# A state-space layer's small tables made on GpSimd instead of VectorE

## The chip, the cores and the metric

One core of a Trainium2 chip runs the whole kernel. TensorE (PE; PEld is its weight load) multiplies, VectorE (DVE) and ScalarE (ACT) do elementwise work, GpSimd (POOL) does little in the kernel before, and SyncE (SP) issues most DMAs; ACT and POOL issue some too. The metric is the device time of one execution in microseconds (us), the median of the runs.

## The reference

Two layers of a streaming encoder over 256 frames of 2048 channels: a diagonal state-space layer (S5), a gated MLP with a causal convolution, attention with a compressed K/V, and a second MLP. The change touches the first of them. Cut to that:

```python
def s5_mixer(u, a_re, a_im, log_dt, b_re, b_im, c_re, c_im, d_skip, w_glu, b_glu):
    dt = exp(log_dt)                        # one per group; 128 groups of 16 channels
    ab = exp(dt * a_re) * (cos(dt * a_im), sin(dt * a_im))   # 64 complex states per group
    bb = (ab - 1) / a * b
    # per group: x_t = bb u_t;  h_t = ab h_{t-1} + x_t;  y_t = Re(c h_t) + d_skip u_t
    y = gelu(y)
    val, gate = split(y @ w_glu + b_glu)    # w_glu is 2048 x 4096
    return val * sigmoid(gate)

h = rmsnorm(x, norm_g[0, 0]);  x = x + rmsnorm(s5_mixer(h, ...), norm_g[0, 1])
```

All arithmetic is float32 (products of weights as a high and a low part, so that each weight tile is split first: `whi` by ScalarE, `wlo` by VectorE).

## The kernel before

`s5` treats the 256 frames as 32 chunks of 8. Within a chunk the recurrence is a small matrix per group; from chunk to chunk a scan runs over the state. The 128 groups go in 16 blocks of 8 groups, and a loop of 18 rounds (`for n in range(nb + 2)`) pipelines the blocks: in round n, block n is prepared (`part_k`, `part_e`), block n - 1 has its scan (`part_v`, `part_r`, `part_h`) and block n - 2 gives its output (`part_c`). Four blocks make a quarter. At the end of a quarter `part_d` takes the Gelu, and a list `todo` of early GLU units (1 MB of weights each, `glu_early`) is worked off by `advance` between the parts.

What the change touches:

- `scale_x(rs, qt)`: x of quarter qt. VectorE multiplies both halves by the norm's weights `gX` (L369), ScalarE then by the rows' norms `rs` into `Xn` (L373). x lies in two tiles of the tag `raw`, into which the first two GLU weight units are loaded later (L84).
- `powers(qt)`: for a quarter's 32 groups, the eight powers of the complex step `L`, three doublings of four VectorE instructions each (L396 to L399) in the tile `z`; ScalarE then writes the signed copies `zs` (L401 to L404).
- `product` (L453): `zs` times the weights `bc` of a block, four 128x1024 VectorE instructions, two for `e` and two for `f`. The two of e are added by an accumulating DMA that POOL issues (L467).
- `frames(k)`: phase tables of two blocks. VectorE reduces the angle (L411 to L413), ScalarE takes Abs, Sin and Sin (L414 to L416). `part_r` and `part_h` multiply by them.
- the skip weights `dB` times a mask (L352), which `part_k` adds (L437).
- `rstd` (L117): the first norm; POOL takes the power -0.5 (L121).
- `lead_e(n)` and `lead_f(n)` make e and f of a block one or two rounds ahead. At the end of round n stand `lead_f(n + 1)` and `lead_e(n + 2)`.

Each engine works through its own queue in order. A scheduler sets the order when the program is built, from the order of the code and modelled times; `behind(ins)` places what is written in it behind the instruction `ins` of the same engine. A tile with a tag shares its tag's buffers, so an instruction also waits for the buffer's last reader.

Of the kernel before, what the change touches and what calls it, by code (L numbers as in the profile page):

```python
# [11 lines left out]
AF = mybir.ActivationFunctionType  # L12
# [3 lines left out]
P = 128  # L16
# [30 lines left out]
def tile_trunk(ctx: ExitStack, tc: tile.TileContext, a: dict):  # L47
# [69 lines left out]
    def rstd(tot, width, n):  # L117
        ms = T(sp, [P, width], F32, "rs_ms")
        dve.tensor_scalar(ms, tot, 1.0 / n, EPS, op0=ALU.mult, op1=ALU.add)
        y = T(sp, [P, width], F32, "rs_y")  # L120
        pool.tensor_tensor(y, ms, eps_half[:, :width], op=ALU.pow)  # L121
# [62 lines left out]
    def behind(ins):  # L184
        return nullcontext() if ins is None else tc.issue_after(ins)
# [96 lines left out]
    def s5(f):  # L282
        with tc.tile_pool(name="s5", bufs=2) as q1, tc.tile_pool(name="dr", bufs=2, space=bass.MemoryType.DRAM) as dr:
            w0 = env["wp"]
            dt = T(q1, [P, P], F32, "dt", 1)
            sA = T(q1, [P, 2, P], F32, "sA", 1)
            sync.dma_start(sA, a["sA"])
            sync.dma_start(dt, a["sL"].partition_broadcast(P))
            sync.dma_start(cst, a["cst"])
            X = [T(w0, [P, 4, 512], F32, "raw") for _ in range(2)]  # L290
            for k in range(8):
# [60 lines left out]
            dve.tensor_tensor(  # L352
                dB.rearrange("p (g q) -> p g q", q=16),
                dB.rearrange("p (g q) -> p g q", q=16),
                dmask.unsqueeze(1).to_broadcast([P, 32, 16]),
                op=ALU.mult,
            )

            def first_norm():
                pst = wk()  # L360
# [2 lines left out]

            Xn = [T(aa, [P, 8, P], F32, f"act{q}") for q in range(4)]

            def scale_x(rs, qt):
                c = slice(P * qt, P * qt + P)
                for h in range(2):
                    dve.tensor_tensor(  # L369
                        X[h][:, :, c], X[h][:, :, c], gX[:, c].unsqueeze(1).to_broadcast([P, 4, P]), op=ALU.mult  # L370
                    )
                for s in range(8):
                    act.activation(  # L373
                        Xn[qt][:, :, 16 * s : 16 * s + 16],
                        X[s // 4][:, s % 4, c].rearrange("p (g q) -> p g q", q=16),
                        AF.Copy,
                        scale=rs[:, s : s + 1],
                    )

            def powers(qt):  # L380
                ps_ = slice(32 * qt, 32 * qt + 32)
                z = T(q1, [P, 2, 9, 2, 32], F32, "z", 1)
                pool.memset(z[:, 0, 8, 1, :], 1.0)
                pool.memset(z[:, 1, 8, 1, :], 0.0)
                act.activation(z[:, :, 8, 0, :], cf[:, :, ps_], AF.Copy)
                act.activation(z[:, :, 0, 1, :], L[8][:, :, ps_], AF.Copy)
                for k, o, i, m in ((1, 7, 8, 1), (2, 5, 7, 2), (4, 1, 5, 4)):

                    def v(b):
                        return z[:, :, b : b + m].rearrange("p c m t n -> p c (m t) n")  # L390

                    def l(c):
                        return L[k][:, c, ps_].unsqueeze(1).unsqueeze(1).to_broadcast([P, 2, 2 * m, 32])

                    u, w = (T(q1, [P, 2, 8, 32], F32, n, 1)[:, :, : 2 * m, :] for n in ("pu", "pw"))
                    dve.tensor_tensor(u, v(i), l(0), op=ALU.mult)  # L396
                    dve.tensor_tensor(w, v(i), l(1), op=ALU.mult)
                    dve.tensor_tensor(v(o)[:, 0], u[:, 0], w[:, 1], op=ALU.subtract)
                    dve.tensor_tensor(v(o)[:, 1], u[:, 1], w[:, 0], op=ALU.add)  # L399
                zz = T(q1, [P, 4, 8, 32], F32, "zs")  # L400
                act.activation(zz[:, 1], z[:, 1, 0:8, 1, :], AF.Copy, scale=cst[:, C_SG : C_SG + 1])  # L401
                act.activation(zz[:, 2], z[:, 0, 1:9, 0, :], AF.Copy, scale=cst[:, C_NSG : C_NSG + 1])
                act.activation(zz[:, 3], z[:, 1, 1:9, 0, :], AF.Copy, scale=-1.0)
                act.activation(zz[:, 0], z[:, 0, 0:8, 1, :], AF.Copy)  # L404
                return zz

            def frames(k):
                ps_ = slice(FR * NP * k, FR * NP * (k + 1))
                m, n = T(q1, [P, FR * NP, 32], F32, "si"), T(q1, [P, FR * NP, 32], F32, "co")
                cv = cst[:, C_CV : C_CV + 32].unsqueeze(1).to_broadcast([P, FR * NP, 32])  # L410
                dve.tensor_tensor(m, th[:, ps_].unsqueeze(2).to_broadcast([P, FR * NP, 32]), cv, op=ALU.mult)  # L411
                dve.tensor_scalar(n, m, MAGIC, MAGIC, op0=ALU.add, op1=ALU.subtract)
                dve.tensor_tensor(m, m, n, op=ALU.subtract)  # L413
                act.activation(n, m, AF.Abs)  # L414
                act.activation(m, m, AF.Sin, scale=cst[:, C_TPI : C_TPI + 1])
                act.activation(n, n, AF.Sin, bias=half_pi, scale=-TWO_PI)  # L416
                return [z.rearrange("p (k n) c -> k p (n c)", k=FR) for z in (m, n)]

            FR = 2
# [41 lines left out]
            def lead_e(n):  # L461
                if n >= nb:
                    return
                if n % PB == 0:
                    zs[n // PB] = powers(n // PB)
                E[n], e2 = product("e1", 3, n, 0), product("e2", 2, n, 1)
                pool.dma_start(E[n], e2, accum_op=ALU.add)  # L467

            def lead_f(n):
                if n >= nb:  # L470
                    return
                F[n] = product("f1", 3, n, 2), product("f2", 3, n, 3)
                if n % FR == 0:
                    si, co = frames(n // FR)
                    for k in range(FR):
                        fr[n + k] = (si[k], co[k])

# [30 lines left out]
            def part_e(e1):  # L508
                ET = T(q1, [P, NP, P], F32, "ET", 1)
                for w in range(NG):  # L510
                    ptv = wk().rearrange("p (g t) -> p g t", g=4)
                    for g in range(4):
                        pe.transpose(ptv[:, g, :], e1[:, 4 * w + g].rearrange("p s q -> p (s q)"), ident)
                    act.activation(ET[:, 4 * w : 4 * w + 4, :], ptv, AF.Copy)
                return ET

            def part_v(U, ET):
# [80 lines left out]
            def advance(steps):  # L598
                for _ in range(steps):
                    while todo and next(todo[0], True) is True:  # L600
                        todo.pop(0)

            rs = first_norm()
            for n in range(3):
                fetch(n, sync)
            lead_e(0)
            lead_f(0)
            scale_x(rs, 0)
            for n in range(nb + 2):
                if 0 <= n - 1 < nb:  # L610
                    vs = part_v(U[n - 1], ET.pop(n - 1))
                if n >= 2:
                    m = n - 2
                    if m % PB == 0:
                        yg = T(q1, [P, 8, P], F32, "yg", 1)
                    part_c(m, yg, F.pop(m), U.pop(m), TP.pop(m), H.pop(m))
                if 0 <= n - 1 < nb:
                    R = part_r(n - 1, vs, *fr[n - 1])
                if n < nb:
                    U[n], TP[n] = part_k(n, F[n], bc.pop(n))  # L620
                    fetch(n + 3, act)
                    ET[n] = part_e(E.pop(n))
                if n > nb:
                    advance(2)
                if n >= 2 and m % PB == PB - 1:
                    part_d(m // PB, yg)
                    todo.append(glu_steps(m // PB))
                if n <= nb:
                    advance(2)
                    if n == nb:  # L630
                        tiny = T(sp, [P, 1], F32, "tot")
                        act.activation(tiny, half_pi, AF.Gelu_apprx_tanh)
# [12 lines left out]
        return todo  # L645
# [595 lines left out]
```

## Time and profile before

| | |
|---|---|
| time, median of 3 runs | 2130.54 us (2128.49 to 2135.25) |
| profiled execution | 2132.15 us, of which the span is 2130.4 us |
| TensorE busy | 2048.3 us (96%) |
| VectorE busy | 1375.3 us (65%) |
| ScalarE busy | 1092.4 us (51%) |
| GpSimd busy | 31.4 us (1%) |
| granted TensorE clock, mean | 0.991 |

The span runs from the first to the last instruction. A row of a timeline reads: start, length (of all if "xN" stands behind), engine and line, operation, output<-inputs with their shapes, and in brackets the idle time of the engine ahead of it and what ended that. A row of groups has the number of instructions, then busy us in all, mean ns of one, and idle time. A row of waits has who waited <- for whom, then us in all, times, and the longest.

### The profile page before, as it was taken

Reading aid. Unit: us, or ns where it says so; the run is one execution under the profiler, and the core shown is the slowest. Engines: PE = TensorE matmul, PEld = TensorE weight load, DVE = VectorE, ACT = ScalarE, POOL = GpSimd, SP = SyncE. Lnnn points to the kernel's source line nnn. Section 1 sums busy time; section 2 is a strip of 40 time slices with the busy share of each in tenths; the row PEclk is TensorE's granted clock in tenths of the full one; section 3 lists DMA queues with packets and bytes.
Section 4 is the critical chain, followed back from the end, with each engine's and each line's share of the span. In section 5 each row is a group of like instructions: output and inputs, shape, how many; then the busy total and the mean of one; then the engine's idle time right before and its main releaser. Section 6 shows DMA issues by size and latency. Waiting matters only on the chain.

```text
span 2130.4 us, 30733 instructions
## 1 busy us (share of the span) xinstructions
PE 2048.3 (96%) x12372; PEld 1755.5 (82%) x12372; DVE 1375.3 (65%) x1931; ACT 1092.4 (51%) x1676; POOL 31.4 (1%) x73
## 2 busy tenths in 40 slices
PE   3789999999999999999999999999999999999998
PEld 2567788988888888888878998898888888888886
DVE  8889677665466556656685666666546655665567
ACT  6565456554455345434464555555445544553444
POOL 1000000000000000000000000000000000000000
PEclk9899999999999999999999999999999999999999
DMA  5768775455655565555564344445555556555554
GB/s 149 202 182 212 247 249 167 154 184 183 201 188 185 190 198 183 181 190 197 197 198 149 124 139 165 168 161 186 179 200 194 185 185 201 182 193 182 198 190 147
DMA packets 292255, 392.15 MB, mean 184 GB/s; under 512 B 10256, under 2 KB 205456, under 8 KB 291600
## 3 DMA queue, kind: packets, MB, share of 16 engines
q1 hardware_dynamic: 285632, 374.45, 53.4%
q0 software_dynamic: 2304, 8.39, 2.3%
q10 hardware_dynamic: 4176, 7.34, 1.0%
q8 instruction: 97, 1.59, 0.3%
q14 instruction: 46, 0.38, 0.1%
HBM read 375.73 MB, written 6.03 MB: 179 GB/s over the span
## 4 chain that ended last, share of the span: by engine, by line
PE 85%; DVE 6%; DMA 4%; ACT 2%; issue 1%; SPq 0%; POOL 0%; ACTq 0%; DVEq 0%; POOLq 0%
PE wk L757 29%; PE wk L759 15%; PE acc L114 9%; PE acc L113 9%; PE acc L112 9%; PE wk L112 2%; PE wk L113 2%; PE wk L114 2%; PE wk L430 2%; PE acc L254 2%; PE acc L253 2%; PE acc L256 1%; DVE wlo L76 1%; ACT junk L139 1%; PE acc L193 1%
## 5 line engine op out<-in xcount | busy, mean ns | idle before, releaser
L76 DVE TENSOR_TENSOR wlo<-raw,whi 128x1024 fp32r<-128x1024 f32 (+1 forms) x606 | 719.4, 1190 | 568.1 <-ACT whi L75 562.9
L75 ACT ACTIVATE whi<-raw 128x1024 fp32r<-128x1024 f32 (+1 forms) x606 | 622.6, 1030 | 708.2 <-PE wk L757 311.3
L757 PE MATMUL wk<-act,whi 128*128 128x512 f32 x2688 | 673.7, 392 | 0.0
L757 PEld LDWEIGHTS wk<-act,whi 128*128 128x128 f32 x2688 | 484.0, 189 | 86.9
L759 PEld LDWEIGHTS wk<-act,wlo 128*128 128x128 f32 x2688 | 366.7, 190 | 26.2
L759 PE MATMUL wk<-act,wlo 128*128 128x256 f32 x2688 | 374.8, 282 | 0.0
L114 PE MATMUL acc<-whi,hl 128*128 128x512 f32 x652 | 255.9, 394 | 0.0
L113 PE MATMUL acc<-wlo,hh 128*128 128x512 f32 x652 | 255.8, 392 | 0.0
L112 PE MATMUL acc<-whi,hh 128*128 128x512 f32 x652 | 253.5, 389 | 0.0
L113 PEld LDWEIGHTS acc<-wlo,hh 128*128 128x128 f32 x652 | 122.4, 188 | 28.3 <-DVE wlo L76 0.2
L112 PEld LDWEIGHTS acc<-whi,hh 128*128 128x128 f32 x652 | 122.4, 188 | 27.5 <-ACT hh L75 0.5
L114 PEld LDWEIGHTS acc<-whi,hl 128*128 128x128 f32 x652 | 122.6, 188 | 24.7
L816 DVE SCALAR_TENSOR_TENSOR cv<-gs,cw,cv 128x255 f32<-128x255 f32 (+1 forms) x168 | 81.0, 482 | 17.2 <-ACT cv L814 14.3
L814 ACT ACTIVATE cv<-gs,cb,cw 128x256 f32<-128x256 f32 x84 | 49.9, 594 | 45.9 <-DVE gs L765 45.9
L253 PE MATMUL acc<-whi,act 128*128 128x512 f32 x156 | 65.3, 419 | 3.9 <-ACT act L75 3.8
L254 PE MATMUL acc<-whi,act 128*128 128x512 f32 x156 | 63.1, 404 | 1.2 <-DVE act L76 1.2
L113 PE MATMUL acc<-wlo,act 128*128 128x512 f32 (+1 forms) x152 | 54.6, 359 | 0.1
L112 PE MATMUL acc<-whi,act 128*128 128x512 f32 (+1 forms) x152 | 54.0, 357 | 0.0
L114 PE MATMUL acc<-whi,act 128*128 128x512 f32 (+1 forms) x152 | 53.9, 356 | 0.0
L112 PE MATMUL wk<-x,whi 128*128 128x256 f32 x160 | 47.2, 297 | 2.3 <-ACT x L75 2.3
L256 PE MATMUL acc<-wlo,act 128*128 128x512 f32 x156 | 49.1, 397 | 0.0
L76 DVE TENSOR_TENSOR x<-raw,x 128x1024 fp32r<-128x1024 f32 x30 | 36.0, 1221 | 16.2 <-ACT x L75 16.2
(306 smaller groups left out, 2503.3 us busy)
## 6 DMA issues: line engine op xcount, KB each, us to landing
raw<-in_w_gate SPq DMA_DIRECT2D x88, 1024.0 KB
raw<-in_w_up SPq DMA_DIRECT2D x88, 1024.0 KB
raw<-in_w_down SPq DMA_DIRECT2D x88, 1024.0 KB
raw<-in_w_glu SPq DMA_DIRECT2D x21, 1024.0 KB
x<-in_w_glu SPq DMA_DIRECT2D x11, 1024.0 KB
raw<-in_w_o SPq DMA_DIRECT2D x9, 1024.0 KB
e<-e POOLq DMA_DIRECT2D x16, 512.0 KB, 6.1
TP<-kd SPq DMA_DIRECT2D x64, 128.0 KB
```

Source lines behind the costliest of these rows:

```text
L75: act.activation(hi, src, AF.Copy)
L76: (eng or dve).tensor_tensor(lo, src, hi.bitcast(F32), op=ALU.subtract)
L112: pe.matmul(o, lh, rh, start=first, stop=False)
L113: pe.matmul(o, lh, rl, start=False, stop=False)
L114: pe.matmul(o, ll, rh, start=False, stop=last)
L253: pe.matmul(bank, ah, wh[:, k, :], start=first and k == 0, stop=False)
L254: pe.matmul(bank, al, wh[:, k, :], start=False, stop=False)
L256: pe.matmul(bank, acts(tb, 4 * b + j + k)[0], wl[:, k, :], start=False, stop=last and k == hk - 1)
L757: pe.matmul(o, w, pair(kt), start=kt == 0, stop=False)
L759: pe.matmul(o[:, 0, :], w, pair(kt)[:, 0], start=False, stop=kt == KT - 1)
L814: act.activation(cv[:, ft, :], gv[:, ft, :], AF.Identity, scale=cw[:, 2, n : n + 1], bias=cb[:, n : n + 1])
L816: dve.scalar_tensor_tensor(cv[:, ft, sh:], gv[:, ft, : S - sh], cw[:, 2 - sh, n : n + 1], cv[:, ft, sh:], op0=ALU.mult, op1=ALU.add,)
```

## The change

- The phase tables' angles (`angles`, from L411 to L413), the powers of quarters 1 to 3 counted from 0, and the multiplication of x by `gX` for those quarters go to POOL, and so does the mask of the skip weights. Quarter 0's powers and multiplication stay on VectorE.
- On POOL they are placed behind the last accumulating DMA issued so far (`env["trig"]`; the first two tables behind nothing, what follows them behind the norm's power).
- The first two tables are made ahead of the norm. Otherwise angles are made in `lead_f`, and ScalarE's sines for them in `lead_r`, a round later; powers of a quarter are made in rounds 0, 2 and 6, ScalarE's copies (`signs`) in rounds 2, 6 and 10, behind the last copy of ET.
- ScalarE scales quarters 1, 2 and 3 of x in rounds 2, 3 and 4, before in rounds 0 and 1.
- The tiny Gelu that is written near the end of the layer (it loads ScalarE's table) is placed behind the last sine.
- The step `dt` is loaded ahead of `sA`.

The diff, cut to its core:

```diff
-        pool.tensor_tensor(y, ms, eps_half[:, :width], op=ALU.pow)
+        env["trig"] = pool.tensor_tensor(y, ms, eps_half[:, :width], op=ALU.pow).ins
...
+            sync.dma_start(dt, a["sL"].partition_broadcast(P))
             sync.dma_start(sA, a["sA"])
-            sync.dma_start(dt, a["sL"].partition_broadcast(P))
...
+            def gain_x(qt, eng):
+                c = slice(P * qt, P * qt + P)
+                with behind(env["trig"] if eng is pool else None):
+                    for h in range(2):
+                        z = X[h][:, :, c]
+                        eng.tensor_tensor(z, z, gX[:, c].unsqueeze(1).to_broadcast([P, 4, P]), op=ALU.mult)
...
-            def powers(qt):
+            def powers(qt, eng):
...
-                    dve.tensor_tensor(u, v(i), l(0), op=ALU.mult)
-                    dve.tensor_tensor(w, v(i), l(1), op=ALU.mult)
-                    dve.tensor_tensor(v(o)[:, 0], u[:, 0], w[:, 1], op=ALU.subtract)
-                    dve.tensor_tensor(v(o)[:, 1], u[:, 1], w[:, 0], op=ALU.add)
+                    eng.tensor_tensor(u, v(i), l(0), op=ALU.mult)
+                    eng.tensor_tensor(w, v(i), l(1), op=ALU.mult)
+                    eng.tensor_tensor(v(o)[:, 0], u[:, 0], w[:, 1], op=ALU.subtract)
+                    eng.tensor_tensor(v(o)[:, 1], u[:, 1], w[:, 0], op=ALU.add)
+                return z
...
-            def frames(k):
+            def angles(k):
...
-                dve.tensor_tensor(m, th[:, ps_].unsqueeze(2).to_broadcast([P, FR * NP, 32]), cv, op=ALU.mult)
-                dve.tensor_scalar(n, m, MAGIC, MAGIC, op0=ALU.add, op1=ALU.subtract)
-                dve.tensor_tensor(m, m, n, op=ALU.subtract)
+                with behind(env.get("trig")):
+                    pool.tensor_tensor(m, th[:, ps_].unsqueeze(2).to_broadcast([P, FR * NP, 32]), cv, op=ALU.mult)
+                pool.tensor_scalar(n, m, MAGIC, MAGIC, op0=ALU.add, op1=ALU.subtract)
+                pool.tensor_tensor(m, m, n, op=ALU.subtract)
+                return m, n
...
-                pool.dma_start(E[n], e2, accum_op=ALU.add)
+                env["trig"] = pool.dma_start(E[n], e2, accum_op=ALU.add).ins
...
+            an = {k: angles(k) for k in range(2)}
             rs = first_norm()
+            with behind(env["trig"]):
+                skips = dB.rearrange("p (g q) -> p g q", q=16)
+                pool.tensor_tensor(skips, skips, dmask.unsqueeze(1).to_broadcast([P, 32, 16]), op=ALU.mult)
+            gain_x(1, pool)
+            gain_x(2, pool)
...
+                        with behind(env["sin"]):
+                            act.activation(tiny, half_pi, AF.Gelu_apprx_tanh)
...
+                if n % PB == 2 and n + 2 < nb:
+                    zs[n // PB + 1] = signs(z)
                 lead_e(n + 2)
-                if n < 2:
-                    scale_x(rs, n + 1)
+                if n == 0 or n % PB == 2 and n + 6 < nb:
+                    z = powers((n + 6) // PB, pool)
                 if n == 1:
-                    scale_x(rs, 3)
+                    gain_x(3, pool)
+                if 1 < n < 5:
+                    scale_x(rs, n - 1)
```

The order that results, at three places. Row: line, operation, output<-inputs, shape; numbers behind names count tiles. The lines of the changed kernel are some 20 higher. First POOL's queue after the memsets at the program's start, before:

```order
L121 TENSOR_TENSOR rs_y_205<-rs_ms_203,cst_73 128x8
L383 MEMSET z_577 128x32
L384 MEMSET z_577 128x32
L467 DMA e_71_247<-e_72_249 128x1024
L467 DMA e_86_323<-e_87_325 128x1024
L467 DMA e_90_332<-e_91_334 128x1024
```

And the same place now:

```order
L414 TENSOR_TENSOR si_200<-th_179,cst_73 128x512
L414 TENSOR_TENSOR si_205<-th_179,cst_73 128x512
L415 TENSOR_SCALAR co_201<-si_200 128x512
L415 TENSOR_SCALAR co_206<-si_205 128x512
L416 TENSOR_TENSOR si_200<-si_200,co_201 128x512
L416 TENSOR_TENSOR si_205<-si_205,co_206 128x512
L121 TENSOR_TENSOR rs_y_214<-rs_ms_212,cst_73 128x8
L615 TENSOR_TENSOR dB_107<-dB_107,cst_73 128x512
L365 TENSOR_TENSOR raw_96<-raw_96,gX_106 128x4x128
L365 TENSOR_TENSOR raw_97<-raw_97,gX_106 128x4x128
L365 TENSOR_TENSOR raw_96<-raw_96,gX_106 128x4x128
L365 TENSOR_TENSOR raw_97<-raw_97,gX_106 128x4x128
```

Two tables now stand ahead of the norm's power, and the skip weights and two quarters of x between it and the first DMA of e. Next VectorE, from the last steps of the first norm to the first product, before:

```order
L127 TENSOR_TENSOR rs_r_211<-rs_t_207,rs_y_205 128x8
L399 TENSOR_TENSOR z_219<-pu_230,pw_231 128x128
L369 TENSOR_TENSOR raw_97<-raw_97,gX_106 128x4x128
L396 TENSOR_TENSOR pu_236<-z_219,L_34_148 128x512
L397 TENSOR_TENSOR pw_237<-z_219,L_34_148 128x512
L369 TENSOR_TENSOR raw_96<-raw_96,gX_106 128x4x128
L398 TENSOR_TENSOR z_219<-pu_236,pw_237 128x256
L399 TENSOR_TENSOR z_219<-pu_236,pw_237 128x256
L369 TENSOR_TENSOR raw_97<-raw_97,gX_106 128x4x128
L453 TENSOR_TENSOR f_73_252<-zs_242,bc_213 128x1024
```

And the same end now:

```order
L127 TENSOR_TENSOR rs_r_220<-rs_t_216,rs_y_214 128x8
L396 TENSOR_TENSOR z_233<-pu_238,pw_239 128x64
L397 TENSOR_TENSOR z_233<-pu_238,pw_239 128x64
L394 TENSOR_TENSOR pu_244<-z_233,L_33_147 128x2x128
L395 TENSOR_TENSOR pw_245<-z_233,L_33_147 128x2x128
L396 TENSOR_TENSOR z_233<-pu_244,pw_245 128x128
L397 TENSOR_TENSOR z_233<-pu_244,pw_245 128x128
L394 TENSOR_TENSOR pu_250<-z_233,L_34_148 128x512
L395 TENSOR_TENSOR pw_251<-z_233,L_34_148 128x512
L396 TENSOR_TENSOR z_233<-pu_250,pw_251 128x256
L397 TENSOR_TENSOR z_233<-pu_250,pw_251 128x256
L459 TENSOR_TENSOR f_77_266<-zs_256,bc_227 128x1024
```

Of the multiplications by `gX` none stands here any more, and the norm's end stands earlier among the powers. Last ScalarE at its start (L632 is the tiny Gelu; L139 the squares of x for the norm), before:

```order
L306 ACTIVATE dt_91<-dt_91 128x128
L632 ACT_TABLE_LOAD
L632 ACTIVATE tot_2761<-cst_73 128x1
L311 ACT_TABLE_LOAD
L311 ACTIVATE mag_117<-e_18_115 128x128
L312 ACTIVATE mag_20_118<-e_18_115 128x128
L139 ACTIVATE junk_122,xst_21_121<-raw_96 128x512
```

And now:

```order
L306 ACTIVATE dt_91<-dt_91 128x128
L139 ACTIVATE junk_122,xst_21_121<-raw_96 128x512
L311 ACTIVATE mag_117<-e_18_115 128x128
L312 ACTIVATE mag_20_118<-e_18_115 128x128
L139 ACTIVATE junk_124,xst_21_121<-raw_96 128x512
```

Two table loads have left the start; the Gelu's now stands behind the sines of the last table.

More of the change, by code (lines that the diff above doesn't have):

```diff
@@ L351, in s5 @@
             dmask = cst[:, C_DM : C_DM + 16]
[L352 to L357, printed above, removed]
             def first_norm():
@@ L378, in scale_x @@
                     )
-            def powers(qt):
+            def powers(qt, eng):
                 ps_ = slice(32 * qt, 32 * qt + 32)
                 z = T(q1, [P, 2, 9, 2, 32], F32, "z", 1)
-                pool.memset(z[:, 0, 8, 1, :], 1.0)
+                with behind(env["trig"] if eng is pool else None):
+                    pool.memset(z[:, 0, 8, 1, :], 1.0)
                 pool.memset(z[:, 1, 8, 1, :], 0.0)
@@ L395, in powers, with signs @@
                     u, w = (T(q1, [P, 2, 8, 32], F32, n, 1)[:, :, : 2 * m, :] for n in ("pu", "pw"))
[L396 to L399, printed above, removed]
-                zz = T(q1, [P, 4, 8, 32], F32, "zs")
[L401 to L404, printed above, removed]
+                    eng.tensor_tensor(u, v(i), l(0), op=ALU.mult)
[3 more added lines that the diff above has]
+                return z
+            def signs(z):
+                zz = T(q1, [P, 4, 8, 32], F32, "zs")
+                with behind(env.get("et")):
+                    act.activation(zz[:, 1], z[:, 1, 0:8, 1, :], AF.Copy, scale=cst[:, C_SG : C_SG + 1])
+                    act.activation(zz[:, 2], z[:, 0, 1:9, 0, :], AF.Copy, scale=cst[:, C_NSG : C_NSG + 1])
+                    act.activation(zz[:, 3], z[:, 1, 1:9, 0, :], AF.Copy, scale=-1.0)
+                    act.activation(zz[:, 0], z[:, 0, 0:8, 1, :], AF.Copy)
                 return zz
-            def frames(k):
+            def angles(k):
                 ps_ = slice(FR * NP * k, FR * NP * (k + 1))
@@ L472, in lead_f, with lead_r @@
                 F[n] = product("f1", 3, n, 2), product("f2", 3, n, 3)
-                if n % FR == 0:
-                    si, co = frames(n // FR)
+                if n % FR == 0 and n // FR > 1:
+                    an[n // FR] = angles(n // FR)
+            def lead_r(n):
+                if n < nb and n % FR == 0:
+                    si, co = frames(*an.pop(n // FR))
                     for k in range(FR):
@@ L513, in part_e @@
                         pe.transpose(ptv[:, g, :], e1[:, 4 * w + g].rearrange("p s q -> p (s q)"), ident)
-                    act.activation(ET[:, 4 * w : 4 * w + 4, :], ptv, AF.Copy)
+                    env["et"] = act.activation(ET[:, 4 * w : 4 * w + 4, :], ptv, AF.Copy).ins
                 return ET
@@ L601, in advance @@
                         todo.pop(0)
+            an = {k: angles(k) for k in range(2)}
             rs = first_norm()
+            with behind(env["trig"]):
[3 more added lines that the diff above has]
+            gain_x(2, pool)
             for n in range(3):
                 fetch(n, sync)
+            zs[0] = signs(powers(0, dve))
             lead_e(0)
             lead_f(0)
+            gain_x(0, dve)
             scale_x(rs, 0)
@@ L622, in s5 @@
                     ET[n] = part_e(E.pop(n))
+                    lead_r(n)
                 if n > nb:
```

10 lines of the change are left out of this document (2 added, 8 removed).

## Prediction

> **What bounds the kernel now.** I read the head of the page first, then a table of busy time by stage, then who waited for whom in the stage that the change touches.
>
> ```profile
> span 2130.4 us, 30733 instructions
> PE 2048.3 (96%) x12372; PEld 1755.5 (82%) x12372; DVE 1375.3 (65%) x1931; ACT 1092.4 (51%) x1676; POOL 31.4 (1%) x73
> ```
>
> Over the whole span TensorE is the bound: it is idle for 2130.4 - 2048.3 = 82.1 us in all, and no change on other engines can win more than that. The stage table (columns after the stretch: its length, then busy us and instructions of PE, PEld, DVE, ACT, POOL, the granted clock, DMA share, GB/s) shows where these idle us lie.
>
> ```profile
> 0.00:25.40 25.40, 0.59 (x2) 0.50 (x2) 18.97 (x57) 18.49 (x45) 3.30 (x17) 1.00 0.48 157
> 25.40:60.00 34.60, 21.57 (x296) 15.60 (x300) 30.58 (x49) 16.92 (x51) 3.84 (x6) 0.90 0.71 178
> 60.00:100.00 40.00, 28.07 (x346) 21.14 (x339) 34.47 (x56) 23.99 (x47) 3.66 (x6) 0.83 0.69 185
> 100.00:126.00 26.00, 24.84 (x360) 20.65 (x358) 24.98 (x35) 18.15 (x39) 1.92 (x4) 1.00 0.73 191
> 126.00:140.00 14.00, 9.10 (x101) 7.28 (x99) 8.10 (x12) 5.86 (x11) 0.86 (x1) 0.94 0.69 178
> 140.00:200.00 60.00, 55.67 (x707) 44.09 (x708) 59.54 (x98) 38.93 (x72) 3.48 (x4) 0.96 0.76 204
> 200.00:235.00 35.00, 35.00 (x431) 28.56 (x431) 27.23 (x42) 16.32 (x31) 1.01 (x3) 1.00 0.61 169
> ```
>
> All of the change lies in these 235 us (the state-space layer with the early GLU units), and so do 60.2 of the 82.1 us: 24.8, 13.0, 11.9, 1.2, 4.9, 4.3 and 0. VectorE is the engine to look at: it is busy for 157.7 of the 174.6 us from 25.4 to 200, and for all but 1.5 us of the two stretches 100 to 126 and 140 to 200, while POOL does almost nothing. After 200 TensorE has no idle time and VectorE has some: there nothing is to be won.
>
> The waits of TensorE in this stage name VectorE (the steps of R, H and f), but also ACT at the start:
>
> ```profile
> PE wk L482 <- ACT act L373: 6.3, 1, 6.3
> PE wk L545 <- DVE R L540: 6.3, 3, 5.3
> PE wk L430 <- DVE H L554: 5.5, 1, 5.5
> PE wk L430 <- DVE f L453: 4.6, 2, 2.8
> PE wk L513 <- DMA e<-e: 2.6, 1, 2.6
> ```
>
> **What leaves VectorE.** These groups are the phase tables (L411 to L413), the powers (L396 to L399), x times its gain (L369) and the skip weights (L352):
>
> ```profile
> L396 DVE TENSOR_TENSOR pu<-z,L 128x128 f32<-128x128 f32 (+2 forms) x12 | 5.6, 464 | 0.1
> L397 DVE TENSOR_TENSOR pw<-z,L 128x128 f32<-128x128 f32 (+2 forms) x12 | 5.6, 464 | 0.0
> L411 DVE TENSOR_TENSOR si<-th,cst 128x512 f32<-128x512 f32 x8 | 5.4, 685 | 0.0
> L369 DVE TENSOR_TENSOR raw<-raw,gX 128x512 f32<-128x512 f32 x8 | 5.4, 685 | 0.0
> L413 DVE TENSOR_TENSOR si<-si,co 128x512 f32<-128x512 f32 x8 | 5.4, 680 | 0.0
> L398 DVE TENSOR_TENSOR z<-pu,pw 128x64 f32<-128x64 f32 (+2 forms) x12 | 3.7, 308 | 0.1
> L399 DVE TENSOR_TENSOR z<-pu,pw 128x64 f32<-128x64 f32 (+2 forms) x12 | 3.7, 306 | 0.0
> L412 DVE TENSOR_SCALAR co<-si 128x512 f32<-128x512 f32 x8 | 3.3, 420 | 0.0
> L352 DVE TENSOR_TENSOR dB<-dB,cst 128x512 f32<-128x512 f32 x1 | 0.7, 686 | 0.0
> ```
>
> Tables 0 and 1 stand ahead of VectorE's wait for ScalarE's first sines:
>
> ```profile
> 9.44 1.29 DVE L411 TENSOR_TENSOR si<-th,cst 128x512 f32<-128x512 f32 x2
> 12.62 0.43 DVE L321 TENSOR_TENSOR L<-L,mag 128x256 f32<-128x256 f32 x1
> ```
>
> All tables: 14.1 us. Three quarters of the powers: 0.75 x 18.6 = 14.0 us. Six of eight multiplications by the gain: 4.1. With the skip weights that makes 32.9 us in 24 + 36 + 6 + 1 = 67 instructions. Tables 0 and 1 (a quarter of 14.1, 3.5 us) are made before 12.62 us, inside that wait, and save nothing: 29.4 us in 61 instructions remain. Instructions that follow each other overlap by some 0.08 us (two products take 2.35 us in the next fence, not twice 1.22), so the room that VectorE gains is 29.4 - 61 x 0.08, about 24.5 us.
>
> **What it costs on POOL.** No row shows large arithmetic on POOL. Its memsets do show a fixed part and a rate:
>
> ```profile
> 0.74 0.31 POOL L651 MEMSET krE<- 128x256 f32 x1 [0.29 <-POOLq L1231]
> 1.83 0.12 POOL L383 MEMSET z<- 128x32 f32 x1
> 19.58 1.76 POOL L121 TENSOR_TENSOR rs_y<-rs_ms,cst 128x8 f32<-128x8 f32 x1 [17.50 <-DVE rs_ms L119]
> 27.84 2.35 DVE L453 TENSOR_TENSOR e<-zs,bc 128x1024 f32<-128x1024 f32 x2
> 35.55 1.97 PE L513 MATMUL wk<-cst,e 128*128 128x128 f32 x8 [2.55 <-DMA e<-e]
> ```
>
> That is (0.31 - 0.12) / 224 = 0.85 ns an element and about 0.1 us. A tensor_tensor moves three streams where a memset moves one. So the lower bound of a 128x512 one is 0.53 us, as one stream, and the upper, three streams in turn, 1.4 us (a tensor_scalar 0.97). The moved work is 67 instructions with 12288 elements per partition in tables, 3 x 2688 in powers, 3072 in gains and 512: 23936. Lower bound 6.7 + 20.3 = 27 us; upper 6.7 + 0.85 x (3 x 19840 + 2 x 4096) = 64 us. I take a value near the upper, 55 us, since two reads and a write are nearer to three streams than to one. The power of L121 is another operation and no price for a product.
>
> [...]
>
> POOL has the room: it is busy for 18 of the 235 us. Behind the moved work in its queue stand the sixteen accumulating DMAs of e. The powers of a quarter, some 7 us, stand ahead of one of them. TensorE waited for an e only once, 2.6 us at the first; the others land ahead of use. I cost this at nothing; the cover is that lead, and were it gone, up to 7 us would be lost in each of three quarters. ScalarE's sines come a round later, still ahead of the product that reads them: nothing again. That x is kept longer (ScalarE scales quarter 3 three rounds later) moves the first two 1 MB loads of GLU weights, which are loaded into the tiles of x. In the run before, they stand right behind a TP transfer that then takes long:
>
> ```profile
> 47.52 2.44 SPq L502 DMA_DIRECT2D TP<-kd  x4
> 50.07 3.28 SPq L84 DMA_DIRECT2D raw<-in_w_glu  x2
> 49.38 8.91 DMA TP<-kd
> 127.34 10.08 DMA bc<-in_sBC
> ```
>
> This collision goes and comes back a round or two later, where every round has one (the wait for bc at 127 is such a case, and stays): nothing, with 4 us to either side in the range.
>
> **Where the room on VectorE turns into time.** Start: of the six multiplications by the gain that stand ahead of the first products of e, two remain: 4 x 0.6 = 2.4 us, and the first transposes of e at 35.55 follow: -2.4. I count nothing for the two table loads that leave ScalarE's start (it then waits for POOL's first table), nor for the swapped first loads, a few tenths. From 25.4 to 100 some 8 of the 24.5 us go, in a chain that passes from VectorE to TensorE, ScalarE and the TP transfer and back; TensorE is idle for 24.9 us there, and I take half of the 8: -4. From 100 to 200 some 12 us go, but TensorE is idle for only 1.2 + 4.3 = 5.5 us beside the wait for bc, which caps it; I take -4. The tail: the Gelu table is loaded earlier, out of the path:
>
> ```profile
> 235.29 1.28 ACT L581 ACT_TABLE_LOAD   x1
> 237.27 1.18 PE L585 MATMUL wk<-cst,yg 128*128 128x128 f32 x8 [0.85 <-ACT yg L581]
> ```
>
> TensorE's wait there is 0.85 us: -1 with what follows it. Sum: -2.4 - 4 - 4 - 1 = -11.4 us, from the profiled execution's 2132.15 to 2120.7. That execution is 1.6 us above the median of 2130.54, so in terms of the median 2119.
>
> **The row on which the sign hangs.** Do POOL and VectorE get in each other's way? There is one kind of row that tells: POOL's small power beside VectorE instructions.
>
> ```profile
> 1383.46 1.21 DVE L76 TENSOR_TENSOR wlo<-raw,whi 128x1024 fp32r<-128x1024 f32 x1
> 1383.68 1.39 POOL L147 TENSOR_TENSOR rs_y<-tot,cst 128x1 f32<-128x1 f32 x1 [16.03 <-DVE tot L145]
> 1384.65 1.21 DVE L76 TENSOR_TENSOR wlo<-raw,whi 128x1024 fp32r<-128x1024 f32 x1
> 1390.43 0.54 POOL L147 TENSOR_TENSOR rs_y<-tot,cst 128x1 f32<-128x1 f32 x1 [5.31 <-DVE tot L145]
> ```
>
> The same instruction takes 0.54 us alone and 1.39 us when it begins inside a VectorE instruction with two SBUF inputs: it ends 0.40 us after that one. So they do exclude each other, and here POOL gave way: both VectorE instructions keep their 1.21 us. My forecast reads this as the rule: POOL, which has time, fits into VectorE's pauses and its PSUM reads.
>
> [...]
>
> **Rivals.** (1) VectorE waits for whole POOL instructions, and the kernel gets slower. Place: from 21 us (skip weights and gains beside the first powers) to 200. Price: VectorE loses 0.9 of POOL's time (its busy share, 157.7 of 174.6) and wins 24.5. Without the first two tables, of which most runs before 12.6 us, POOL has 24 to 56 us: between -3 and +26 us on VectorE. At my 55 us, 48 remain: +19, of which the chain's pauses before 100 us take up some 7: +12, so 2142.5. It decides from the point where a 128x512 instruction on POOL holds VectorE for longer than about 0.65 us, what VectorE needs for it.
> (2) The relief is hidden: TensorE runs at 93 to 96% from 100 us on, the TP and bc transfers set the rounds before, and the start gains nothing, since rs then comes late. Only the tail and 1 or 2 us remain: 2127. For it speaks that the biggest single wait (bc, 10.08 us) is a DMA's; against it that VectorE is busy without a break for 100 us.
> (3) VectorE really was behind most of TensorE's idle time: all but the 4.9 us around the bc wait of the 35.3 us from 25.4 to 200 shrinks by two thirds, with start and tail: -24, so 2107.
>
> **How the numbers follow.** Forecast 0.38 (its own range 2113 to 2124); rival 1 0.27; rival 2 0.25; rival 3 0.10. A difference within 0.3%, 6.4 us, is about what cannot be told from no change. Faster is forecast and rival 3, with a hundredth from rival 2: 0.49. Slower is rival 1 but for two hundredths: 0.25. Same is the rest: 0.26. The range reaches from 2106 (rival 3) to 2143 (rival 1 at its taken price), which leaves out its upper half and the rest of rival 3, below 0.2.
>
> **What would show it.** Right: the stretch up to the last early part (235 us now) shorter by about 10 us, VectorE below 90% from 100 to 200, its products still 1.22 us and following each other at 1.13, POOL's 128x512 instructions long (over 1 us) and stretched by waiting. Wrong by rival 1: products or wlo well above 1.22 us, or gaps between them that end with POOL. Wrong by rival 2: VectorE with more idle time and TensorE's waits unchanged, now on TP, bc or ACT. A late e or a late first weight would show as a new wait of TensorE for L513, or of ScalarE for raw.

## The result: 1.2% slower

The changed kernel takes 2156.01 us (median of 2154.83 to 2157.94) against 2130.21 us before in runs beside it: a ratio of 1.0116, 95% interval 1.0101 to 1.0132. The forecast was 2119, a gain. The change loses 25.8 us, and the time lies 13 us beyond rival 1.

The head of the page of the changed kernel:

```profile
span 2153.3 us, 30743 instructions
PE 2054.5 (95%) x12372; PEld 1762.1 (82%) x12372; DVE 1387.1 (64%) x1864; ACT 1087.3 (50%) x1672; POOL 117.2 (5%) x140
```

VectorE has 67 instructions fewer, which took 32.9 us, and yet is busy for 11.8 us more (1387.1 against 1375.3): the rest of its work has grown by some 44.7 us. POOL has gained 85.8 us, where 55 were reckoned.

TensorE works off the same 12372 matmuls. Of the 22.9 us by which the profiled span is longer (2153.3 against 2130.4), 16.7 are its idle time (98.8 against 82.1) and 6.2 its busy time (2054.5 against 2048.3); its mean granted clock is 0.985, before 0.991. The sum of the prediction had no term for the clock.

Four of the seven stages, in the cuts of the prediction:

```profile
60.00:100.00 40.00, 26.23 (x418) 20.46 (x406) 38.73 (x41) 22.97 (x54) 28.38 (x25) 0.83 0.77 197
100.00:126.00 26.00, 23.95 (x282) 18.79 (x280) 21.92 (x26) 16.06 (x32) 6.62 (x9) 0.87 0.66 169
126.00:140.00 14.00, 10.33 (x86) 8.42 (x90) 14.00 (x14) 7.53 (x14) 13.84 (x13) 0.76 0.75 209
140.00:200.00 60.00, 47.00 (x534) 36.79 (x527) 45.64 (x59) 30.56 (x58) 13.63 (x10) 0.91 0.62 161
```

From 60 to 100 us VectorE is now busier (38.73 of 40 us, before 34.47) with fewer instructions (41, before 56). From 126 to 140 VectorE and POOL have no pause between them: 14.00 and 13.84 of 14 us. From 140 to 200 TensorE loses 8.7 us (47.00, before 55.67), and there VectorE is not full. The granted clock is lower in the last three rows than in the same stretches before: 0.87, 0.76 and 0.91, where it was 1.00, 0.94 and 0.96. Apart from the clock, two things are to be told from each other: stretched instructions, and something else that delays TensorE late in the layer.

Which instructions grew, from the groups of VectorE in the first 300 us (busy us, then mean ns of one, then idle time before them):

```profile
L459 DVE TENSOR_TENSOR f<-zs,bc 128x1024 f32<-128x1024 f32 x32 | 45.4, 1420 | 0.2 <-ACT zs L404 0.2
L76 DVE TENSOR_TENSOR wlo<-raw,whi 128x1024 fp32r<-128x1024 f32 x30 | 43.8, 1466 | 11.1 <-ACT whi L75 10.9
L542 DVE TENSOR_TENSOR w<-w,w 128x256 f32<-128x256 f32 x16 | 12.8, 801 | 0.1
L540 DVE TENSOR_TENSOR w<-wk,co 128x256 f32<-128x256 f32 x16 | 6.7, 416 | 4.4 <-PE wk L538 4.4
L279 DVE TENSOR_TENSOR f<-acc,f 128x512 f32<-128x512 f32 x24 | 16.5, 687 | 13.4 <-PE acc L256 13.4
```

The same groups before:

```profile
L453 DVE TENSOR_TENSOR f<-zs,bc 128x1024 f32<-128x1024 f32 x32 | 38.9, 1217 | 0.8 <-PE wk L430 0.8
L76 DVE TENSOR_TENSOR wlo<-raw,whi 128x1024 fp32r<-128x1024 f32 x32 | 39.0, 1221 | 8.2 <-ACT whi L75 8.1
L534 DVE TENSOR_TENSOR w<-w,w 128x256 f32<-128x256 f32 x16 | 6.7, 421 | 0.1
L532 DVE TENSOR_TENSOR w<-wk,co 128x256 f32<-128x256 f32 x16 | 6.7, 421 | 6.1 <-PE wk L530 6.1
L279 DVE TENSOR_TENSOR f<-acc,f 128x512 f32<-128x512 f32 x24 | 16.5, 687 | 8.6 <-PE acc L256 8.6
```

Instructions with both operands in SBUF (f from zs and bc, wlo, w from w and w) grew by 17%, 20% and 90%. Those with one operand in PSUM (`wk`, `acc` are PSUM tiles) kept their length to within 0.005 us: 416 against 421 ns, 687 against 687. In order of time it looks like this (start, duration, both in us; `x4` is four instructions in a row, with the length of all four):

```profile
24.22 5.75 POOL L365 TENSOR_TENSOR raw<-raw,gX 128x512 f32<-128x512 f32 x4
24.41 1.22 DVE L124 TENSOR_TENSOR rs_t<-rs_t,rs_ms 128x8 f32<-128x8 f32 x1
25.75 1.22 DVE L125 TENSOR_SCALAR rs_t<-rs_t 128x8 f32<-128x8 f32 x1
...
59.54 2.82 POOL L365 TENSOR_TENSOR raw<-raw,gX 128x512 f32<-128x512 f32 x2
59.89 2.76 DVE L542 TENSOR_TENSOR w<-w,w 128x256 f32<-128x256 f32 x1
```

At 59.89 an addition that takes 0.42 us before takes 2.76 and ends 0.29 us after POOL's two multiplications. An instruction of eight elements per partition takes 1.22 us beside POOL's multiplications (24.41 and 25.75), before 0.16. Here it is VectorE that gives way.

The second suspect is in the waits of the first 300 us (total us, times, longest):

```profile
ACT co L420 <- POOL si L416: 25.4, 6, 6.0
PE wk L490 <- ACT act L370: 10.3, 1, 10.3
PE wk L553 <- DVE R L548: 9.3, 3, 4.1
PE wk L521 <- ACT yg L574: 7.7, 2, 4.8
PE wk L521 <- ACT U L492: 4.5, 2, 4.4
```

ScalarE waits 25.4 us for POOL's tables, six times. In its queue its copies for `yg` and `U` stand behind that `Abs` (L420), and TensorE then waits 7.7 and 4.5 us for them. How the wait arises can be seen at 153:

```profile
153.14 0.87 POOL L471 DMA_DIRECT2D e<-e  x1 [12.68 <-issue]
153.70 1.62 POOL L414 TENSOR_TENSOR si<-th,cst 128x512 f32<-128x512 f32 x1
155.41 2.78 POOL L415 TENSOR_SCALAR co<-si 128x512 f32<-128x512 f32 x1
158.27 1.26 POOL L416 TENSOR_TENSOR si<-si,co 128x512 f32<-128x512 f32 x1
159.57 0.63 ACT L420 ACTIVATE co<-si 128x512 f32<-128x512 f32 x1 [5.99 <-POOL si L416]
```

The table stands in POOL's queue behind the trigger of an accumulating DMA that POOL issues only at 153.14, then takes 5.8 us, and ScalarE has come to it 6 us too early.

### The profile page after: what moved, and what is told of

Read it like the earlier page. It is cut to its first block, busy times and chain, and to the rows that moved or that the text cites. A ratio compares the mean times of both kernels' runs of the same rounds, so it can differ in the third digit from the quotient of the medians.

```text
span 2153.3 us, 30743 instructions
## 1 busy us (share of the span) xinstructions
PE 2054.5 (95%) x12372; PEld 1762.1 (82%) x12372; DVE 1387.1 (64%) x1864; ACT 1087.3 (50%) x1672; POOL 117.2 (5%) x140
## 4 chain that ended last, share of the span: by engine, by line
PE 83%; DVE 4%; DMA 2%; ACT 2%; issue 1%; SPq 0%; POOL 0%; ACTq 0%; DVEq 0%; POOLq 0%
PE wk L779 28%; PE wk L781 15%; PE acc L114 9%; PE acc L113 9%; PE acc L112 9%; PE wk L112 2%; PE wk L113 2%; PE wk L114 2%; PE acc L253 1%; PE acc L254 1%; DVE wlo L76 1%; PE acc L256 1%; DMA bias<-in_b_glu 1%; PE wk L256 1%; PE acc L193 1%
## 5 line engine op out<-in xcount | busy, mean ns | idle before, releaser
L147 POOL TENSOR_TENSOR rs_y<-tot,cst 128x1 f32<-128x1 f32 x18 | 12.8, 713 | 1914.1 <-DVE tot L145 1190.9
```

## Experiments

Three theories. T1: VectorE and POOL keep each other out of SBUF, so that VectorE loses more than the moved work gave it. T2: the stretch is harmless, and ScalarE's wait in its queue for POOL's tables is the loss. T3: the new order alone (sines a round later, x scaled later, Gelu table, first loads) is the loss.

**All arithmetic back on VectorE, the new order kept** (all_dve). The edit, on the changed kernel, cut to its lines:

```diff
-                with behind(env.get("trig")):
-                    pool.tensor_tensor(m, th[...], cv, op=ALU.mult)
-                pool.tensor_scalar(n, m, MAGIC, MAGIC, op0=ALU.add, op1=ALU.subtract)
-                pool.tensor_tensor(m, m, n, op=ALU.subtract)
+                dve.tensor_tensor(m, th[...], cv, op=ALU.mult)
+                dve.tensor_scalar(n, m, MAGIC, MAGIC, op0=ALU.add, op1=ALU.subtract)
+                dve.tensor_tensor(m, m, n, op=ALU.subtract)
...
-            gain_x(1, pool)
-            gain_x(2, pool)
+            gain_x(1, dve)
+            gain_x(2, dve)
...
-                    z = powers((n + 6) // PB, pool)
+                    z = powers((n + 6) // PB, dve)
```

> The changed kernel with all of its POOL arithmetic put back on VectorE (tables, powers, gains, skip weights); the new order, the later sines, the Gelu table's place and the swapped first loads stay. Theory 1 (VectorE and POOL exclude each other, the stretch of VectorE's instructions is the loss) and theory 2 (ScalarE waits in its queue for POOL's tables) both expect 2124 to 2131 us, at or a little below the kernel before, with products back at 1.22 us. Theory 3 (the new order itself costs: x kept longer, first GLU weights later) expects more than 2140.

Measured: 2131.21 us, ratio to before 1.0005 (0.9991 to 1.002). T3 falls: the new order costs nothing that can be measured, and gains nothing.

**Only the tables back on VectorE** (angles_dve: the first half of that diff), and **only the tables on POOL** (angles_only: its second half).

> Only the phase tables go back to VectorE; powers, gains and skip weights stay on POOL. POOL then has 45 of its 86 us of moved work. Theory 1 expects about half of the loss to stay, 2138 to 2146 us, with products still stretched. Theory 2 (ScalarE's waits for tables, 25.4 us in six) expects the whole loss but the start's part to be gone: 2130 to 2136.

> Only the phase tables stay on POOL (41 of the 86 us); powers, gains and skip weights go back to VectorE. Theory 1 expects 2138 to 2146 us. Theory 2 expects ScalarE's waits to stay near 20 us and the time near 2150.

Measured: 2140.79 us, ratio 1.0053 (1.0036 to 1.007), with powers, gains and skip weights on POOL; 2156.07 us, ratio 1.013 (1.0105 to 1.0154), with the tables alone. The tables by themselves give a loss as large as the whole change, the rest 9 us; the two parts do not add up (24 + 9 against 25). ScalarE's wait for POOL is 23.9 us in angles_only and absent in angles_dve, so these two runs still fit T2 for the larger part, but not T2 alone: angles_dve has no such wait and is slower all the same. T1's 2138 to 2146 holds for angles_dve and is missed by 10 us for angles_only.

**The start back on VectorE** (start_dve).

```diff
-            an = {k: angles(k) for k in range(2)}
+            an = {k: angles(k, dve) for k in range(2)}
...
-            gain_x(1, pool)
-            gain_x(2, pool)
+            gain_x(1, dve)
+            gain_x(2, dve)
```

(The skip weights go back too.)

> The changed kernel with the work ahead of the first round on VectorE again: the first two tables, the skip weights and the gains of quarters 1 and 2. The first transposes of e came 7.1 us later with the change (42.64 against 35.55 us). If that delay runs through to the end, the time falls by 6 to 9 us to 2147 to 2150, and the first transposes come before 36. If it is taken up by later waits, the time stays within 2 us of 2156.

Measured: 2149.03 us, ratio 1.009 (1.0074 to 1.0106), 7 us less than the changed kernel. In all these kernels the transposes of e (eight per block, 128 in all) are a mark of how far the layer has come. Their row in the view by source line gives count, shortest/median/longest ns, and the first and last start; one row each of before, changed, all_dve, angles_dve, angles_only and start_dve:

```profile
L513 PE MATMUL wk<-cst,e x128: 272/273/473, 35.6 to 220.1; 128*128 128x128 f32 x128
```
```profile
L521 PE MATMUL wk<-cst,e x128: 272/273/477, 42.6 to 244.5; 128*128 128x128 f32 x128
```
```profile
L520 PE MATMUL wk<-cst,e x128: 272/273/477, 41.7 to 218.0; 128*128 128x128 f32 x128
```
```profile
L520 PE MATMUL wk<-cst,e x128: 272/273/476, 38.3 to 229.8; 128*128 128x128 f32 x128
```
```profile
L521 PE MATMUL wk<-cst,e x128: 272/273/476, 47.6 to 244.4; 128*128 128x128 f32 x128
```
```profile
L521 PE MATMUL wk<-cst,e x128: 272/273/476, 35.9 to 238.7; 128*128 128x128 f32 x128
```

The last start gives each kernel's delay: +24.4, -2.1, +9.7, +24.3 and +18.6 us, which are the differences in time within 3 us. All of the loss arises up to there, in the layer. The first start is no such measure: all_dve begins 6.1 us late and has made it up by the end, start_dve begins on time and ends 18.6 late.

**ScalarE's Abs a round later** (late_sines). It takes T2's cause away: the Abs is queued behind ScalarE's last copy of transposes, and POOL's work stays. **The same with the start on VectorE** (start_late, with start_dve's edit of the start; its text counts the quarters from 1).

```diff
-                act.activation(n, m, AF.Abs)
+                with behind(env.get("et")):
+                    act.activation(n, m, AF.Abs)
```

> The changed kernel, with one order changed: ScalarE's Abs on a table, and so the two sines, is put behind the last copy of e transposes that was issued before it, about a round later in ScalarE's queue; all work on GpSimd stays. Theory T2 (ScalarE waits in its in-order queue for GpSimd's tables): of the 25.4 us that ScalarE waits for them some 20 lie behind the start and go; time 2133 to 2140. Theory T1 (VectorE and GpSimd exclude each other): VectorE's stretch of some 45 us stays as it is, and with it the loss: 2150 to 2158. Both: between, about 2142 to 2148, with ScalarE's wait under 8 us.

> The changed kernel with the first two tables, the skips and the gains of quarters 2 and 3 on VectorE (start_dve, measured at 2149.0) and ScalarE's Abs a round later (as in late_sines). Theory T2: start and waits repaired, nothing is left of the loss: 2128 to 2134. Theory T1: the stretch of VectorE's instructions beside GpSimd's powers and 14 later tables stays, worth 9 us or more by the kernel with only the tables back (2140.8): 2140 to 2149.

Measured: 2152.54 us, ratio 1.0104 (1.0087 to 1.012), and 2146.86 us, ratio 1.0072 (1.0056 to 1.0087). ScalarE's wait for POOL's tables is gone altogether (25.4 us to none), and the time falls by 3.5 us, which the intervals do not separate from nothing; with the start on VectorE it is 2.2 us. T2 had asked for 16 to 23. In late_sines the waits have another name:

```profile
ACT dc L545 <- DVE R L549: 24.1, 8, 8.3
PE wk L554 <- DVE R L549: 19.8, 8, 8.0
```

TensorE and ScalarE now wait for VectorE's scan (in the changed kernel TensorE's wait for it was 9.3 us). The scan's mean is 952 ns, 761 in the changed kernel and 686 before; the products of f have 1533 ns, 1420 and 1217. ScalarE's early wait had stood in front of this one; taking it away showed the next. T2 names a true wait, but its removal by itself is worth little.

**The disputed cost by itself.** Kernels from before, in which POOL gets work that nobody reads and nobody waits for, behind the trigger of each of the first 14 accumulating DMAs: six multiplications of 128x256 (pool_reads), twelve memsets (pool_writes), three multiplications (pool_half), three tensor_scalar with one SBUF input (pool_scalar).

```diff
-                pool.dma_start(E[n], e2, accum_op=ALU.add)
+                last = pool.dma_start(E[n], e2, accum_op=ALU.add).ins
+                for _ in range(6 if n < 14 else 0):
+                    with behind(last):
+                        last = pool.tensor_tensor(sc, cst[:, 0:256], cst[:, 256:512], op=ALU.mult).ins
...
+            sc = T(q1, [P, 256], F32, "spare", 1)
```

> The kernel before, with 84 GpSimd multiplications of 128x256 added (six behind each of the first 14 accumulating transfers, of constants into a spare tile that nobody reads; all else unchanged, no engine waits for them). Theory T1: VectorE's instructions with two SBUF operands wait for whole GpSimd instructions: 84 x 0.5 to 0.9 us = 40 to 75 us of GpSimd, VectorE's busy time up by 15 to 45 us, time 2138 to 2155; 128x1024 products up from 1.22 us, PSUM-reading 128x256 unchanged at 0.42. Theory T2: nobody waits for them, so 2126 to 2134, and VectorE's means as before.

> The kernel before, with 168 GpSimd memsets of 128x256 added (twelve behind each of the first 14 accumulating transfers, into a spare tile), about 50 us of GpSimd time as in pool_reads, but without an SBUF input. Theory T1 in its narrow form (the two engines exclude each other on their reads only): VectorE's means as before, 2126 to 2134. Theory T1 in its wide form (any GpSimd access): as pool_reads, 2138 to 2155. Theory T2: 2126 to 2134.

> The kernel before with 42 added GpSimd multiplications of 128x256 (three behind each of the first 14 accumulating transfers instead of the six of pool_reads, which cost 30 us but kept later transfers waiting behind them). If the price is VectorE's waiting: VectorE busy up by 14 to 22 us (half of 38), PE's waits for the accumulating transfers as before (2.6 us, once), time 2140 to 2149. If the 30 us came from the transfers that stood behind the multiplications: no such queue is left, time 2128 to 2136 even though VectorE is stretched.

> The kernel before with 42 added GpSimd tensor_scalar instructions of 128x256 (add and subtract of a constant, one SBUF input; places as in pool_half). If only GpSimd instructions with two SBUF inputs keep VectorE out: VectorE's busy time within 3 us of before, 2126 to 2134. If one input is enough: 42 x 1.0 us of GpSimd, VectorE up by 15 to 30 us, 2138 to 2155.

| kernel | added on POOL | VectorE busy, against 1375.3 | time | ratio |
|---|---|---|---|---|
| pool_reads | 84 multiplications | +38.3 us | 2162.37 | 1.0142 (1.0127 to 1.0157) |
| pool_half | 42 multiplications | +20.1 us | 2144.37 | 1.0061 (1.0044 to 1.0078) |
| pool_scalar | 42 tensor_scalar | +5.8 us | 2136.52 | 1.0024 (1.0014 to 1.0035) |
| pool_writes | 168 memsets | +0.2 us | 2130.39 | 0.9994 (0.9984 to 1.0003) |

Groups, source rows and waits behind the table, of pool_reads, pool_half, pool_scalar and pool_writes in turn:

```profile
L453 DVE TENSOR_TENSOR f<-zs,bc 128x1024 f32<-128x1024 f32 x32 | 46.5, 1457 | 0.4 <-PE wk L430 0.4
L535 DVE TENSOR_TENSOR w<-wk,co 128x256 f32<-128x256 f32 x16 | 6.7, 416 | 3.2 <-PE wk L533 3.2
L470 POOL TENSOR_TENSOR spare<-cst 128x256 f32<-128x256 f32 x84 | 107.2, 1276 | 5.5
```
```profile
L470 POOL TENSOR_TENSOR spare<-cst x42: 722/1064/7444, 31.2 to 189.6; 128x256 f32<-128x256 f32 x42
PE wk L548 <- DVE R L543: 14.8, 6, 6.2
```
```profile
L470 POOL TENSOR_SCALAR spare<-cst x42: 1069/1454/7760, 31.6 to 186.2; 128x256 f32<-128x256 f32 x42
```
```profile
L453 DVE TENSOR_TENSOR f<-zs,bc 128x1024 f32<-128x1024 f32 x32 | 38.9, 1217 | 0.4 <-PE wk L430 0.4
L470 POOL MEMSET spare<- 128x256 f32 x168 | 57.1, 340 | 8.8
PE wk L548 <- DVE R L543: 6.9, 4, 5.4
```

What T1 expects is shown: work on POOL with no reader makes VectorE's two-SBUF instructions longer (the products of f 1457 ns in pool_reads, 1217 before), and the kernel with them, by 12 us for 42 multiplications and 30 for 84 (7 us above the expectation for pool_reads). TensorE's waits for VectorE's scan rise with it, from 6.3 to 14.8 us in pool_half. The PSUM reader L535 has 416 ns in pool_reads, 421 before. Memsets in the same places, 57 us of them against pool_half's 61.5 us of multiplications, change neither the time nor TensorE's waits for the scan (6.9 us) and for the accumulating DMAs (2.6): a busy POOL queue alone cost nothing here, and of the four kernels only the three whose added work reads SBUF made VectorE slower. A multiplication costs VectorE 0.46 to 0.48 us (38.3 / 84, 20.1 / 42), a tensor_scalar 0.14 (5.8 / 42) though it is the longer one on POOL (shortest 1069 against 722 ns). The expectation for pool_scalar missed: 2136.52 lies between its two cases, and the price is small but there. The expectation had gone by POOL's time, and that does not price the collision: POOL is busy for 72.2 us with them, for 61.5 us with pool_half's multiplications. One reservation on pool_reads: its multiplications, stretched, hold up the triggers behind them, and TensorE's waits for accumulating DMAs rise from 2.6 to 8.5 us. In pool_half they are 5.5 us, where 2.6 were expected, so that some 3 of its 12 us may be theirs; it is the cleaner figure. In pool_scalar they are 8.2, and its 4.5 us may be theirs altogether.

Does it matter where POOL works? The same 84 multiplications, all behind the last accumulating DMA, where VectorE is busy for only three quarters of the time (pool_late); and, since that kernel had a wait of its own, again with the spare tile in a pool of its own memory (pool_last).

```diff
-                for _ in range(6 if n < 14 else 0):
+                for _ in range(84 if n == nb - 1 else 0):
```
```diff
-            sc = T(q1, [P, 256], F32, "spare", 1)
+            sc = T(cp, [P, 256], F32, "spare", 1)
```

> The kernel before with the same 84 GpSimd multiplications as pool_reads, but all behind the last accumulating transfer (from about 210 us on), where VectorE is busy for 71 of 100 us and PE for 97. VectorE's instructions are stretched there too (products of weights, 128x1024, above 1.3 us), but it has room: 2128 to 2140. If the price goes with the count of instructions wherever they stand: 2150 to 2165.

> The kernel before with the 84 GpSimd multiplications of pool_late in the same place (behind the last accumulating transfer, from about 200 to 280 us), but with the spare tile in memory of its own. pool_late lost 41 us, and its trace has one wait of 38.9 us of a weight load for memory that GpSimd's last multiplication had to leave first. If that wait was its loss: it goes, VectorE's instructions in that stretch still are up to 1.7 us instead of 1.2, and the time is 2130 to 2138. If the loss was VectorE kept out by a GpSimd that is never idle: 2160 to 2175 again.

pool_late: 2173.23 us, ratio 1.0198 (1.0177 to 1.0218), above both ranges, and no answer to the question: SyncE's queue waited 41.6 us for POOL to finish before it could load a weight tile, and ScalarE for that tile:

```profile
ACT whi L75 <- DMA x<-in_w_glu: 40.4, 2, 38.9
```

pool_last: 2145.34 us, ratio 1.0062 (1.0043 to 1.008). The wait is gone and with it 28 us, but 15.8 us stay, twice what I had expected at most. Two stages, of before and of pool_last:

```profile
240.00:280.00 40.00, 39.16 (x166) 32.03 (x166) 30.86 (x40) 20.74 (x28) 0.00 (x0) 0.96 0.99 336
280.00:320.00 40.00, 39.84 (x176) 32.54 (x175) 28.76 (x30) 22.74 (x26) 0.00 (x0) 1.00 0.67 217
```
```profile
240.00:280.00 40.00, 35.98 (x139) 28.47 (x140) 29.99 (x31) 18.31 (x24) 37.26 (x36) 0.87 0.92 297
280.00:320.00 40.00, 35.89 (x147) 28.22 (x146) 31.11 (x26) 17.00 (x20) 19.80 (x19) 0.96 0.71 227
```

TensorE loses 3.2 and 4.0 us of busy time in them although VectorE is no busier than 31 of 40 us, and its granted clock is 0.87 and 0.96, before 0.96 and 1.00. Between 230 and 330 us pool_last has, as a group and as a wait,

```profile
L76 DVE TENSOR_TENSOR wlo<-raw,whi 128x1024 fp32r<-128x1024 f32 x11 | 15.9, 1450 | 3.6 <-ACT whi L75 3.6
```
```profile
PE wk L256 <- DVE wlo L76: 5.8, 4, 3.3
```

where before has 1222 ns and 0.2 us. A quarter of idle time on VectorE did not cover the stretch: each `wlo` stands between ScalarE's `whi` and TensorE, and TensorE waits for it. These waits are 5.8 of the 15.8 us; how much of the rest is the lower clock no run separates.

## Why the prediction was wrong

**The row on which the sign hangs: the step that failed.** That the two engines exclude each other was read rightly from the power that took 1.39 instead of 0.54 us. That POOL is then the one to give way was taken as the rule from a case in which POOL came second. With work queued on both sides POOL also comes first, and VectorE waits: 0.42 to 2.76 us at 59.89. The forecast's picture, POOL fitting into VectorE's pauses, does occur (in pool_reads six POOL multiplications take 12.32 us from 31.16 on, where the shortest takes 0.72, while VectorE's products run on without a pause to 38.02), but VectorE's instructions wait in their turn (right after, at 42.82, its addition of w and w takes 0.94 us, before 0.42), and that wait the sum had at nothing. The runs show which instructions are concerned: VectorE's PSUM readers stay at 416 and 687 ns in the changed kernel, and beside POOL's memsets the products stay at 1217. They do not show by what rule the turn is given. Two figures no run explains: the longest multiplication of pool_reads and of pool_half takes 7.44 us, six times one of VectorE's products (1.22), and a tensor_scalar, which reads SBUF too and runs longer, takes 0.14 us from VectorE against a multiplication's 0.46. VectorE's waiting stood in the prediction as rival 1 with 0.27, and as a forecast it had the right direction, with half of the loss.

**Rival 1's own size.** It had +12 us in all. Its direction is the one that happened. That VectorE waits for whole POOL instructions was an assumption of mine, and no run shows it: a 128x256 multiplication, 0.72 us on POOL at its shortest, cost VectorE 0.46 to 0.48 us. VectorE's net was to be +19 with pauses that take up 7; measured are +11.8 us of busy time and +25.8 us of time. So the loss is not VectorE's added busy time less its pauses: among the instructions that grow are those for which TensorE waits (its waits for the scan rise from 6.3 to 9.3 us). Of the 13.5 us that it fell short, about 7 are the start, which it did not count; the other 6 no run separates.

**Start: -2.4, measured about +7.** The first transposes of e move from 35.55 to 42.64 us. That shift is no price by itself, since all_dve begins 6.1 us late and loses nothing; the price is what start_dve gives back, 7 us of the time. The gains beside the norm do leave VectorE, but beside POOL's skip weights and gains the norm's four small instructions take 1.22 us each, before 0.16, and ScalarE waits 5.08 us for POOL's first table with the squares of x behind it.

```profile
17.08 0.63 ACT L420 ACTIVATE co<-si 128x512 f32<-128x512 f32 x1 [5.08 <-POOL si L416]
```

The remark that ScalarE "then waits for POOL's first table" stood there, and was costed at nothing.

**POOL's 55 us, measured 85.8.** With VectorE all but idle beside it, a 128x512 tensor_tensor takes 1.03 us, within the bounds of 0.53 to 1.4. The tensor_scalar was wrong by a factor of two:

```profile
9.55 2.05 POOL L414 TENSOR_TENSOR si<-th,cst 128x512 f32<-128x512 f32 x2 [7.50 <-DVE th L343]
11.57 4.05 POOL L415 TENSOR_SCALAR co<-si 128x512 f32<-128x512 f32 x2
```

2.02 us each (the shortest of the eight 1.97), where the upper bound had 0.97: my estimate by streams of data does not price it. More of the excess lies in the powers: their groups sum to 41.5 us, where the upper bound had 24. POOL's own waiting is part of that; one multiplication of 128x512 there has a mean of 1942 ns, against the 1.03 us beside an idle VectorE.

**ScalarE's sines a round later: nothing.** It was not nothing as a wait (25.4 us), but nearly nothing as a price: late_sines removed it for 3.5 us. The cover named held as far as it went: no wait of VectorE for a sine is in the trace. But it did not keep ScalarE's queue from waiting for POOL, and that the price came out near nothing all the same is luck: VectorE's scan was next in line.

**From 25.4 to 200: -8, measured about +18** (start_dve, with the start repaired, is 17.3 us slower than before, and 18.6 late at the last transposes). The room of 24.5 us was given and taken back: 44.7 us of stretch.

**Right.** The two swapped first loads and the table loads that leave the start bring nothing, and neither does the later x: all_dve contains them all and stands at 1.0005. The forecast's 1 us for the Gelu's tail is too little to be told from none: in all_dve TensorE's wait of 0.85 us there is gone, and the time does not show it.

**What stays open.** angles_only is 24 us slower while VectorE's busy time grows by only 4.8 us (without the tables it should have fallen by 14.1), and its first transposes come 12 us late. How much of its loss is stretch on the path, how much ScalarE's wait and how much the start stays open. So does the clock: whether it falls because TensorE idles more or for another reason, no run here shows. No version here beats the kernel before.

## What to carry to other kernels

Moving elementwise work from VectorE to an idle GpSimd was not moving it to a free engine here, where both read SBUF: price each GpSimd instruction by what it takes from VectorE's two-SBUF instructions (0.46 us for a 128x256 multiplication in pool_reads, where VectorE needs 0.42 for an instruction of that shape, so nothing was to be won), and look for work that only writes (168 memsets added 0.2 us to VectorE), or whose VectorE neighbours read PSUM (they kept 416 and 687 ns). A long wait at the head of a queue is a candidate, not a verdict: remove it and see what waits next (late_sines took 25.4 us of one away, and ScalarE's waits for VectorE's scan rose from 5.3 to 24.1 us). Look at single instructions on the path, not at the average load, to see whether an engine has room: in pool_last VectorE is busy for 31 of 40 us, and TensorE waits 5.8 us for `wlo` all the same.

## What the runs showed of the hardware that I had not expected

- The exclusion was seen in both directions: an addition of VectorE took 2.34 us longer beside two POOL multiplications (59.89 us of the changed kernel), and six POOL multiplications, 0.72 us each at the shortest, took 12.32 us from 31.16 in pool_reads, where VectorE's products follow each other without a pause until 38.02. The longest multiplication there took 7.44 us.
- Even VectorE's instructions of 8 elements per partition took 1.22 us beside POOL's multiplications (23.06 to 28.72 us of the changed kernel), before 0.17 at most; one of the four is a tensor_scalar with one SBUF input (VectorE's L125).
- The POOL tensor_scalar held VectorE far less: 0.14 us for each of 42, and at 12.35 us of the changed kernel VectorE's 128x256 instructions kept their 0.41 us beside it.
- On POOL a tensor_scalar with two operations took longer than a tensor_tensor of the same tile: 2.02 against 1.03 us for 128x512 (changed kernel, 11.57 and 9.55), 1.07 against 0.72 for 128x256 at the shortest (pool_scalar and pool_half).
- POOL's memsets of 128x256, 168 of them in 57 us, left VectorE's means at 1217 ns and the time at 0.9994.
